# Two chained matrix products on one Trainium2 core: transposing x by DMA instead of TensorE, with the first products one block ahead

## The chip, the cores and the metric

The kernel runs on one core of one Trainium2 (trn2) chip. The metric is the device time of one execution in microseconds (us). The kernel before was run three times: median 1066.17 us (1066.07 to 1066.21). The profile is of one further execution, taken by the hardware profiler.

## The reference

```python
def setup_inputs():
    batch, m, k, h, n = 16, 512, 768, 3072, 768
    # x (batch, m, k), w1 (k, h), b1 (h), w2 (h, n), all float32, normally distributed

def reference(x, w1, b1, w2):
    y = np.matmul(x, w1) + b1
    y = np.maximum(y, 0)
    return np.matmul(y, w2).astype(np.float32)
```

x is taken as a matrix of 8192 rows by 768. The first product gives 8192 x 3072, bias and ReLU follow, and the second product gives 8192 x 768.

## The kernel before

The 8192 rows are worked in 16 blocks of 512. All operands are turned into bf16 while they are loaded, by DMAs from GpSimd's queue (POOL), which read fp32 in HBM and write bf16 in SBUF. Both weights stay in SBUF: `w1_sb` as 6 slices of 128 input features by 3072, `w2_sb` as 24 slices of 128 by 768. A row `w_sb` in the profile is either of them, `xl` is a loaded tile of x, 128 rows by 768 (196.6 KB in bf16; the profile writes 192 KB), four to a block.

TensorE multiplies along the partitions, so x is needed with its features on the partitions. `transpose_xblock` makes that tile, `xt`: for each of the four `xl` of a block it issues six TensorE transposes of 128 x 128 against the identity `ident` into a PSUM tile `trp` (two buffers), and VectorE (DVE) copies each `trp` into `xt`. In a block that is 24 transposes and 4 copies.

`mm1(xt)` makes 24 groups of 128 output features. A group is 6 matmuls of 128 x 512 into a PSUM tile `mm1p` (two buffers), and ScalarE (ACT) adds the bias, applies ReLU and writes bf16 into `yt`. A block has 144 of these matmuls. `mm2(blk, yt)` makes four groups of 128 rows. Each runs over the 24 slices of `w2_sb`, two matmuls of 128 x 384 a slice, into two PSUM tiles `mm2p`; DVE copies both into `osb`, and SyncE's queue (SP) stores `osb` to HBM. A block has 192 of these matmuls.

The loads of x run two blocks ahead of their use. At the start POOL issues x of block 0, the first six column pieces of w1 (128 columns each), x of block 1, the other 18 pieces of w1, and 24 pieces of w2. There are eight semaphores for POOL's DMAs, used in turn, so that the ninth issue waits for the first to land; the same holds for SP's DMAs with eight of their own. A scheduler sets each engine's order from the order of the code, and may draw single steps forward: in the kernel before it puts one of a block's four transposed tiles into the block ahead of it. Each engine's queue then runs strictly in that order.

The code and its line numbers in the profile:

Of the kernel before, what the change touches and what calls it, by code (L numbers as in the profile page):

```python
# [1 line left out]

# [5 lines left out]

FP32 = mybir.dt.float32
BF16 = mybir.dt.bfloat16  # L10


@with_exitstack
def kernel(
    ctx: ExitStack,
    tc: tile.TileContext,
    x: bass.AP,
    w1: bass.AP,
    b1: bass.AP,
    w2: bass.AP,  # L20
    out: bass.AP,
):
    nc = tc.nc
    P = 128

    xf = x.flatten_outer_dims()
    of = out.flatten_outer_dims()
    M, K = xf.shape
    K2, H = w1.shape
    H2, N = w2.shape  # L30
    assert K2 == K and H2 == H

    KS = K // P
    HS = H // P
    M_BLK = 512
    MSUB = M_BLK // P
    NBLK = M // M_BLK
    NF = 384
    NH = N // NF

    const_pool = ctx.enter_context(tc.tile_pool(name="const", bufs=1))
    w1_sb = const_pool.tile([P, KS, H], BF16)
    w2_sb = const_pool.tile([P, HS, N], BF16)
    b1_sb = const_pool.tile([P, HS], FP32)
    ident = const_pool.tile([P, P], BF16)

    make_identity(nc, ident)

    xload_pool = ctx.enter_context(tc.tile_pool(name="xload", bufs=8))
    xt_pool = ctx.enter_context(tc.tile_pool(name="xt", bufs=3))  # L50
    yt_pool = ctx.enter_context(tc.tile_pool(name="yt", bufs=2))
    osb_pool = ctx.enter_context(tc.tile_pool(name="osb", bufs=6))

    tr_psum = ctx.enter_context(tc.tile_pool(name="trps", bufs=2, space=bass.MemoryType.PSUM))
    mm1_psum = ctx.enter_context(tc.tile_pool(name="mm1ps", bufs=2, space=bass.MemoryType.PSUM))
    mm2_psum = ctx.enter_context(tc.tile_pool(name="mm2ps", bufs=4, space=bass.MemoryType.PSUM))

    w1r = w1.rearrange("(ko ki) h -> ki ko h", ki=P)

    def load_xblock(blk):  # L60
        m0 = blk * M_BLK
        xls = []
        for ms in range(MSUB):
            xl = xload_pool.tile([P, K], BF16, name="xl")
            nc.gpsimd.dma_start(  # L65
                out=xl, in_=xf[m0 + ms * P: m0 + (ms + 1) * P, :])
            xls.append(xl)
        return xls

    def transpose_xblock(xls):  # L70
        xt = xt_pool.tile([P, KS, M_BLK], BF16, name="xt")
        for ms in range(MSUB):
            trp = tr_psum.tile([P, KS, P], BF16, name="trp")
            for k in range(KS):
                nc.tensor.transpose(trp[:, k, :],  # L75
                                    xls[ms][:, k * P:(k + 1) * P], ident)
            nc.vector.tensor_copy(out=xt[:, :, ms * P:(ms + 1) * P], in_=trp)  # L77
        return xt

    def load_w1(ht0, ht1):  # L80
        for ht in range(ht0, ht1):
            nc.gpsimd.dma_start(out=w1_sb[:, :, ht * P:(ht + 1) * P],  # L82
                                in_=w1r[:, :, ht * P:(ht + 1) * P])

    def load_w2(h0, h1):
        for h in range(h0, h1):
            nc.gpsimd.dma_start(out=w2_sb[:, h, :],  # L87
                                in_=w2[h * P:(h + 1) * P, :])

    def mm1(xt):  # L90
        yt = yt_pool.tile([P, HS, M_BLK], BF16, name="yt")
        for ht in range(HS):
            ps = mm1_psum.tile([P, M_BLK], FP32, name="mm1p")
            for k in range(KS):
                nc.tensor.matmul(ps,  # L95
                                 lhsT=w1_sb[:, k, ht * P:(ht + 1) * P],
                                 rhs=xt[:, k, :],
                                 start=(k == 0), stop=(k == KS - 1))
            nc.scalar.activation(out=yt[:, ht, :], in_=ps,  # L99
                                 func=mybir.ActivationFunctionType.Relu,  # L100
                                 bias=b1_sb[:, ht:ht + 1])
        return yt

    def mm2(blk, yt):
        m0 = blk * M_BLK
        for ms in range(MSUB):
            osb = osb_pool.tile([P, N], FP32, name="osb")
            pss = [mm2_psum.tile([P, NF], FP32, tag="mm2", name="mm2p")
                   for _ in range(NH)]
            for h in range(HS):  # L110
                for j in range(NH):
                    nc.tensor.matmul(pss[j],  # L112
                                     lhsT=yt[:, h, ms * P:(ms + 1) * P],
                                     rhs=w2_sb[:, h, j * NF:(j + 1) * NF],
                                     start=(h == 0), stop=(h == HS - 1))
            for j in range(NH):
                nc.vector.tensor_copy(out=osb[:, j * NF:(j + 1) * NF],  # L117
                                      in_=pss[j])
            nc.sync.dma_start(out=of[m0 + ms * P: m0 + (ms + 1) * P, :],
                              in_=osb)  # L120

    xls0 = load_xblock(0)
    nc.sync.dma_start(out=b1_sb, in_=b1.rearrange("(t p) -> p t", p=P))
    load_w1(0, 6)
    xls1 = load_xblock(1)
    load_w1(6, HS)
    load_w2(0, HS)

    xls_next = [xls0, xls1]
    for blk in range(NBLK):  # L130
        xls = xls_next.pop(0)
        xt = transpose_xblock(xls)
        if blk + 2 < NBLK:
            xls_next.append(load_xblock(blk + 2))
        yt = mm1(xt)
        mm2(blk, yt)


# [1 line left out]
_INS = ['x', 'w1', 'b1', 'w2']  # L140
_OUTS = [((16, 512, 768), 'float32')]


# [23 lines left out]
```

## Time and profile before

| | |
|---|---|
| median of three runs | 1066.17 us |
| span of the profiled execution, first to last instruction | 1066.0 us |
| PE (TensorE matmul) busy | 1033.2 us, 97% of the span |
| ACT busy | 265.2 us, 25% |
| DVE busy | 96.9 us, 9% |
| POOL busy | 67.1 us, 6% |
| DMA, mean over the span | 45 GB/s |

The span starts at the core's first instruction and ends after its last. PE is matmuls and transposes, PEld the loading of their stationary operands, which overlaps PE. Bytes of DMA are those written, so a load of x or of a weight reads twice as many from HBM. The mean duration of a matmul in the profile includes the time in which it overlaps its neighbours; the spacing of matmuls is the busy time of a group over its count. In a row of the timeline the first figure is the start, the second the length, and the brackets at the end say how long the engine had been idle and what ended that.

### The profile page before, as it was taken

To read this page: it belongs to the slowest core of one execution; us is meant where nothing else is said; L and a number is where in the kernel's file an instruction comes from. 1 tells how busy PE (TensorE), PEld (TensorE's weight loads), DVE (VectorE), ACT (ScalarE), POOL (GpSimd) and SP (SyncE) were. 2 spreads that over 40 slices of the span, in tenths; PEclk is the share of its full clock that TensorE was granted. 3 is DMA by queue.
4 is the path that set the end of the run, shared out by engine and by line. 5 is a ranking of instruction groups with operands and counts; after the bars stand their busy time and mean duration, and the time that the engine had idled before them with its cause. 6 is when DMAs were issued, how large, how long until landed. Compare 5 with 4: busy or idle time off the path is not lost.

```text
span 1066.0 us, 12515 instructions
## 1 busy us (share of the span) xinstructions
PE 1033.2 (97%) x5760; PEld 551.0 (52%) x5760; DVE 96.9 (9%) x192; ACT 265.2 (25%) x385; POOL 67.1 (6%) x118
## 2 busy tenths in 40 slices
PE   7889999999999999999999999999999999999998
PEld 3344554645546455454555545455464554545554
DVE  1011010110101101020010101101011010100101
ACT  3303205032140412305123050321404214041230
POOL 7510000000000000000000000000000000000000
PEclk9999999999999999999999999999999999999999
DMA  9962030120301202011020201203012020100001
GB/s 158 195 129 60 16 75 1 45 45 15 75 1 45 45 30 60 1 54 37 30 60 15 69 7 43 47 16 74 1 46 45 19 64 1 45 15 31 30 1 60
DMA packets 43844, 48.00 MB, mean 45 GB/s; under 512 B 24336, under 2 KB 35600, under 8 KB 43792
## 3 DMA queue, kind: packets, MB, share of 16 engines
q0 software_dynamic: 31488, 22.03, 14.2%
q1 hardware_dynamic: 12304, 25.18, 6.3%
q8 instruction: 45, 0.74, 0.3%
q14 instruction: 7, 0.06, 0.0%
HBM read 44.05 MB, written 25.17 MB: 65 GB/s over the span
## 4 chain that ended last, share of the span: by engine, by line
PE 91%; DMA 4%; DVE 3%; POOL 1%; issue 0%; DVEq 0%; POOLq 0%
PE mm2p L112 46%; PE mm1p L95 44%; DMA w_sb<-in_w_dram 4%; DVE osb L117 1%; DVE xt L77 1%; POOL w_sb L82 1%; PE trp L75 1%; POOL xl L65 0%; DVEq L162 0%; POOL ident masks.py:199 0%; POOL ident masks.py:197 0%; POOLq masks.py:199 0%; POOLq L151 0%
## 5 line engine op out<-in xcount | busy, mean ns | idle before, releaser
L112 PE MATMUL mm2p<-w_sb,yt 128*128 128x384 bf16 x3072 | 506.2, 327 | 6.8 <-DMA w_sb<-in_w_dram 6.3
L95 PE MATMUL mm1p<-xt,w_sb 128*128 128x512 bf16 x2304 | 502.1, 380 | 3.9 <-DVE xt L77 3.9
L99 ACT ACTIVATE yt<-mm1p,b_sb 128x512 bf16<-128x512 f32 x384 | 263.9, 687 | 759.6 <-PE mm1p L95 759.6
L112 PEld LDWEIGHTS <-yt 128*128 128x128 bf16 x3072 | 301.1, 98 | 211.0 <-issue 12.3
L95 PEld LDWEIGHTS <-w_sb 128*128 128x128 bf16 x2304 | 225.7, 98 | 275.4 <-issue 8.1
L117 DVE COPY osb<-mm2p 128x384 f32<-128x384 f32 x128 | 65.3, 551 | 945.0 <-PE mm2p L112 945.0
L65 POOL DMA_DIRECT2D xl<-in_x_dram x64 | 34.1, 538 | 785.5 <-PE trp L75 780.4
L75 PE MATMUL trp<-ident,xl 128*128 128x128 bf16 x384 | 30.2, 224 | 17.6 <-DVE xt L77 11.2
L75 PEld LDWEIGHTS <-xl 128*128 128x128 bf16 x384 | 24.8, 100 | 23.6 <-issue 13.0
L77 DVE COPY xt<-trp 128x768 bf16<-128x768 bf16 x64 | 32.8, 549 | 20.4 <-PE trp L75 18.6
L82 POOL DMA_DIRECT2D w_sb<-in_w_dram x24 | 19.7, 836 | 5.2 <-DMA w_sb<-in_w_dram 4.6
L87 POOL DMA_DIRECT2D w_sb<-in_w_dram x24 | 12.7, 531 | 10.7 <-DMA w_sb<-in_w_dram 10.7
L99 ACT ACT_TABLE_LOAD x1 | 1.3, 1283 | 6.1 <-DMA b_sb<-in_b_dram 6.1
masks.py:199 POOL TENSOR_SCALAR_AFFINE_SELECT ident<-ident 128x128 bf16<-128x128 bf16 x1 | 0.3, 306 | 0.1
masks.py:197 POOL MEMSET ident<- 128x128 bf16 x1 | 0.2, 205 | 0.3 <-POOLq L151 0.3
L151 POOL MEMSET const-float32-0.0<- 128x1 f32 x1 | 0.1, 99 | 0.2 <-issue 0.2
L151 POOL MEMSET const-bfloat16-1.0<- 128x1 bf16 x1 | 0.1, 103 | 0.0
L151 POOL MEMSET const-uint8-127<- 128x1 uint8 x1 | 0.1, 103 | 0.0
L151 POOL MEMSET const-float32-1.0<- 128x1 f32 x1 | 0.1, 99 | 0.0
## 6 DMA issues: line engine op xcount, KB each, us to landing
out_dram<-osb SPq DMA_DIRECT2D x64, 384.0 KB, 2.3
xl<-in_x_dram POOLq DMA_DIRECT2D x64, 192.0 KB, 5.3
w_sb<-in_w_dram POOLq DMA_DIRECT2D x48, 192.0 KB, 7.8
b_sb<-in_b_dram SPq DMA_DIRECT2D x1, 12.0 KB, 5.3
```

The costliest lines, as they stand in the source:

```text
L65: nc.gpsimd.dma_start(out=xl, in_=xf[m0 + ms * P: m0 + (ms + 1) * P, :])
L75: nc.tensor.transpose(trp[:, k, :], xls[ms][:, k * P:(k + 1) * P], ident)
L77: nc.vector.tensor_copy(out=xt[:, :, ms * P:(ms + 1) * P], in_=trp)
L82: nc.gpsimd.dma_start(out=w1_sb[:, :, ht * P:(ht + 1) * P], in_=w1r[:, :, ht * P:(ht + 1) * P])
L87: nc.gpsimd.dma_start(out=w2_sb[:, h, :], in_=w2[h * P:(h + 1) * P, :])
L95: nc.tensor.matmul(ps, lhsT=w1_sb[:, k, ht * P:(ht + 1) * P], rhs=xt[:, k, :], start=(k == 0), stop=(k == KS - 1))
L99: nc.scalar.activation(out=yt[:, ht, :], in_=ps, func=mybir.ActivationFunctionType.Relu, bias=b1_sb[:, ht:ht + 1])
L112: nc.tensor.matmul(pss[j], lhsT=yt[:, h, ms * P:(ms + 1) * P], rhs=w2_sb[:, h, j * NF:(j + 1) * NF], start=(h == 0), stop=(h == HS - 1))
L117: nc.vector.tensor_copy(out=osb[:, j * NF:(j + 1) * NF], in_=pss[j])
L151: nc = _bacc.Bacc("TRN2", target_bir_lowering=False, num_devices=1)
```

## The change

Four things are changed:

- x of blocks 1 to 15 is transposed by `dma_start_transpose` on SP's queue, from `xl` in SBUF to `xt` in SBUF, four DMAs of 128 x 768 a block. Block 0 is still transposed on TensorE.
- The loop issues `mm1` of block b ahead of `mm2` of block b-1. `yt` has three buffers instead of two.
- w1 is loaded in pieces of 128, 128, 256 and five times 512 columns, all ahead of x of block 1; w2 in six pieces of four slices.
- The x loads and their transposes are still written two blocks ahead of their use.

```diff
-    yt_pool = ctx.enter_context(tc.tile_pool(name="yt", bufs=2))
+    yt_pool = ctx.enter_context(tc.tile_pool(name="yt", bufs=3))
...
+    def xbar_xblock(xls):
+        xt = xt_pool.tile([P, KS, M_BLK], BF16, name="xt")
+        for ms in range(MSUB):
+            nc.sync.dma_start_transpose(
+                out=xt[:, :, ms * P:(ms + 1) * P], in_=xls[ms])
+        return xt
...
     def load_w1(ht0, ht1):
-        for ht in range(ht0, ht1):
-            nc.gpsimd.dma_start(out=w1_sb[:, :, ht * P:(ht + 1) * P],
-                                in_=w1r[:, :, ht * P:(ht + 1) * P])
+        nc.gpsimd.dma_start(out=w1_sb[:, :, ht0 * P:ht1 * P],
+                            in_=w1r[:, :, ht0 * P:ht1 * P])
+
+    w2r = w2.rearrange("(t p) n -> p t n", p=P)
 
     def load_w2(h0, h1):
-        for h in range(h0, h1):
-            nc.gpsimd.dma_start(out=w2_sb[:, h, :],
-                                in_=w2[h * P:(h + 1) * P, :])
+        nc.gpsimd.dma_start(out=w2_sb[:, h0:h1, :], in_=w2r[:, h0:h1, :])
...
     xls0 = load_xblock(0)
     nc.sync.dma_start(out=b1_sb, in_=b1.rearrange("(t p) -> p t", p=P))
-    load_w1(0, 6)
+    load_w1(0, 1)
+    load_w1(1, 2)
+    load_w1(2, 4)
+    for ht in range(4, HS, 4):
+        load_w1(ht, ht + 4)
     xls1 = load_xblock(1)
-    load_w1(6, HS)
-    load_w2(0, HS)
+    for h in range(0, HS, 4):
+        load_w2(h, h + 4)
 
-    xls_next = [xls0, xls1]
-    for blk in range(NBLK):
-        xls = xls_next.pop(0)
-        xt = transpose_xblock(xls)
-        if blk + 2 < NBLK:
-            xls_next.append(load_xblock(blk + 2))
-        yt = mm1(xt)
-        mm2(blk, yt)
+    xts = [transpose_xblock(xls0), xbar_xblock(xls1)]
+    yts = [None] * NBLK
+    for blk in range(NBLK + 1):
+        if blk < NBLK:
+            if blk + 2 < NBLK:
+                xts.append(xbar_xblock(load_xblock(blk + 2)))
+            yts[blk] = mm1(xts[blk])
+        if blk >= 1:
+            mm2(blk - 1, yts[blk - 1])
```

On PE, at the end of a block's second products: in the kernel before, the last two matmuls of `mm2` of block 0 and the first transpose of an `xl` of block 1 (the numbers tell buffers apart).

```order
L112 LDWEIGHTS yt_193
L112 MATMUL mm2p_549<-w2_sb_59,yt_193 128x384
L112 LDWEIGHTS yt_193
L112 MATMUL mm2p_550<-w2_sb_59,yt_193 128x384
L75 LDWEIGHTS xl_104
L75 MATMUL trp_611<-ident_61,xl_104 128x128
```

In the changed kernel, the same two matmuls of `mm2` of block 0 (`yt_169`), and behind them the first of `mm1` of block 2 (`xt_164`).

```order
L118 LDWEIGHTS yt_169
L118 MATMUL mm2p_731<-w2_sb_59,yt_169 128x384
L118 LDWEIGHTS yt_169
L118 MATMUL mm2p_732<-w2_sb_59,yt_169 128x384
L101 LDWEIGHTS w1_sb_58
L101 MATMUL mm1p_798<-xt_164,w1_sb_58 128x512
```

What moved: no transpose and no wait for one of DVE's copies stands between the two kinds of matmul any more; the `LDWEIGHTS` of L101 waits for the four DMAs that fill `xt_164`.

Also on PE, at the end of `mm1` of block 0 in the changed kernel (`xt_118` is x of block 0, `xt_151` that of block 1):

```order
L101 LDWEIGHTS w1_sb_58
L101 MATMUL mm1p_354<-xt_118,w1_sb_58 128x512
L101 LDWEIGHTS w1_sb_58
L101 MATMUL mm1p_376<-xt_151,w1_sb_58 128x512
L101 LDWEIGHTS w1_sb_58
```

In the kernel before, `mm2` of block 0 stands in the place of `mm1p_376`; now `mm1` of block 1 follows at once, and the four DMA transposes of block 1 are due there.

On POOL, the loads at the start, as a difference (`-` before, `+` changed):

```order
 L65 DMA xl<-in_x_dram 128x768 x3
-L82 DMA w_sb<-in_w_dram 128x6x128 x6
+L88 DMA w_sb<-in_w_dram 128x6x128 x2
+L88 DMA w_sb<-in_w_dram 128x6x256
+L88 DMA w_sb<-in_w_dram 128x6x512 x5
 L65 DMA xl<-in_x_dram 128x768 x4
-L82 DMA w_sb<-in_w_dram 128x6x128 x18
-L87 DMA w_sb<-in_w_dram 128x768 x24
+L94 DMA w_sb<-in_w_dram 128x4x768 x6
 L65 DMA xl<-in_x_dram 128x768 x56
```

What moved: x of block 1 (the four `xl` in the middle) now stands behind all of w1 instead of behind a quarter of it.

On SP, the queue before was one load of b1 and the 64 stores. In the changed kernel it begins:

```order
L131 DMA b_sb<-in_b_dram 128x24x1
L73 DMA_TRANSPOSE xt<-xl 128x6x128 x16
L125 DMA out_dram<-osb 128x768 x4
L73 DMA_TRANSPOSE xt<-xl 128x6x128 x4
L125 DMA out_dram<-osb 128x768 x4
```

What moved: the transposes of blocks 1 to 4 stand ahead of the first store, and from there four transposes alternate with four stores. Each waits for its `xl` to land; the first of a block also waits for the `mm1` that last read its `xt` buffer.

## Prediction, made before the changed kernel was run

> **What bounds the kernel now.** I read the page's head and its groups first, then the chain of work that ended last, then the timeline at one block boundary, and then the start with the DMA rates, because there the changed kernel has a new deadline. The head and the groups:
>
> ```profile
> span 1066.0 us, 12515 instructions
> PE 1033.2 (97%) x5760; PEld 551.0 (52%) x5760; DVE 96.9 (9%) x192; ACT 265.2 (25%) x385; POOL 67.1 (6%) x118
> ...
> L112 PE MATMUL mm2p<-w_sb,yt 128*128 128x384 bf16 x3072 | 506.2, 327 | 6.8 <-DMA w_sb<-in_w_dram 6.3
> L95 PE MATMUL mm1p<-xt,w_sb 128*128 128x512 bf16 x2304 | 502.1, 380 | 3.9 <-DVE xt L77 3.9
> ...
> L75 PE MATMUL trp<-ident,xl 128*128 128x128 bf16 x384 | 30.2, 224 | 17.6 <-DVE xt L77 11.2 <-DMA xl<-in_x_dram 6.2
> ```
>
> PE is the bound. The two products take 1008 us of it; the transposes take 30.2 us, and PE is idle 17.6 us just before them. The chain gives the rhythm of a middle block (start, length, what), and its last row the last second product:
>
> ```profile
> 349.01 31.24 PE mm1p L95 x144
> 380.25 31.05 PE mm2p L112 x191
> 411.32 1.02 DVE osb L117 x2
> 413.39 0.57 DVE xt L77
> 414.00 31.24 PE mm1p L95 x144
> ...
> 1030.20 31.05 PE mm2p L112 x191
> ```
>
> From 349.01 to 414.00 a block takes 64.99 us. The boundary close up:
>
> ```profile
> 411.28 0.83 PE L75 MATMUL trp<-ident,xl 128*128 128x128 bf16 x12
> 412.86 0.96 PE L75 MATMUL trp<-ident,xl 128*128 128x128 bf16 x12 [0.74 <-DVE xt L77]
> 414.00 4.26 PE L95 MATMUL mm1p<-xt,w_sb 128*128 128x512 bf16 x19 [0.18 <-DVE xt L77]
> ```
>
> The second products run from 380.25 to 411.28 (31.03 us), then the transposes and their waits for DVE take until 414.00, which is 2.72 us a block in which no product runs. The start has its own losses:
>
> ```profile
> 10.00 0.10 PEld L95 LDWEIGHTS <-w_sb 128*128 128x128 bf16 x1 [0.56 <-DMA w_sb<-in_w_dram]
> 10.36 10.05 PE L95 MATMUL mm1p<-xt,w_sb 128*128 128x512 bf16 x36 [0.65 <-DVE xt L77]
> 17.86 0.69 ACT L99 ACTIVATE yt<-mm1p,b_sb 128x512 bf16<-128x512 f32 x1 [0.61 <-PE mm1p L95]
> 20.25 0.50 PE L75 MATMUL trp<-ident,xl 128*128 128x128 bf16 x6
> 20.61 19.60 PE L95 MATMUL mm1p<-xt,w_sb 128*128 128x512 bf16 x90
> 43.92 2.70 PE L112 MATMUL mm2p<-w_sb,yt 128*128 128x384 bf16 x14
> 62.37 24.10 PE L112 MATMUL mm2p<-w_sb,yt 128*128 128x384 bf16 x137 [1.32 <-DMA w_sb<-in_w_dram]
> 89.02 1.24 PE L95 MATMUL mm1p<-xt,w_sb 128*128 128x512 bf16 x5 [0.18 <-DVE xt L77]
> ```
>
> Block 0's second products start at 43.92 and creep behind the w2 pieces until 62.37; block 1 starts at 89.02, 45.1 us after 43.92, where 31.03 + 2.72 would do.
>
> ```profile
> 0.00:5.00 5.00, 0.00 (x0) 0.00 (x0) 0.00 (x0) 0.00 (x0) 4.05 (x12) 1.00 0.59 41
> 5.00:10.00 5.00, 3.29 (x24) 2.23 (x25) 1.93 (x4) 1.28 (x1) 4.89 (x7) 1.00 1.36 180
> 25.00:30.00 5.00, 5.00 (x25) 2.29 (x24) 0.00 (x0) 2.57 (x5) 3.29 (x4) 1.00 1.82 181
> 50.00:55.00 5.00, 2.81 (x13) 1.18 (x13) 0.00 (x0) 0.00 (x0) 2.70 (x6) 1.00 1.16 207
> 60.00:65.00 5.00, 3.54 (x14) 1.62 (x13) 0.91 (x2) 0.00 (x0) 0.46 (x1) 0.75 1.16 207
> 65.00:70.00 5.00, 5.00 (x30) 2.90 (x28) 0.11 (x1) 0.00 (x0) 0.00 (x0) 0.91 0.45 123
> ```
>
> These are stretches of 5 us; the last three figures are the granted PE clock, the DMA share and GB/s written. Loads run at 181 GB/s while w1 comes in rows of 256 bytes, at 207 while w2 comes in rows of 1536. From 25 to 30 us PE is full beside that traffic, so DMA does not slow its matmuls. After the thin stretch the clock drops (0.75, then 0.91), which costs 5 x 0.25 + 5 x 0.09 = 1.7 us.
>
> **The change, part by part.** The sum is made against the profiled span, 1066.0 us; the median of the runs lies 0.2 above it.
>
> First products of block 0. Their order and first loads stay, so they start at 10.36, with the same slow first matmuls. The hoisted transposes between 20.25 and 20.61 go (0.36 us), so they end at 43.92 - 0.36 = 43.56. The larger w1 pieces could delay them: the fourth piece (columns 4 to 7 of the 24 groups) is needed when the fourth group is done, about 17.6 (its ACT row starts at 17.86). By 10 us 5 x 41 + 5 x 180 = 1105 KB had come; x of block 0 and the first three pieces are 8 tiles' worth, 1573 KB, so they are in at 12.6 by 180 GB/s, and the next 786 KB at 16.4 by 207 or 16.9 by 181. The first w1 piece was byte-wise in at 9.3 and released PE at 10.0, so 0.7 is added: 17.1 to 17.6. That just holds, and the later pieces gain on PE (3.8 to 4.3 us each against 5.2 us of matmuls). I take 0; ends 0 and +1.
>
> x of block 1, and its transposes: this is the term that decides. PE wants `xt` of block 1 at 43.56. All of w1 and x of block 1 are 6.29 MB, in by 12.6 + 4.72 MB / 207 + 0.7 = 36.1 for the last `xl`, and 2.8 earlier, 33.3, for the first. (At 181 GB/s the last lands at 39.4.) The trace before has no DMA transpose. The rows nearest to it:
>
> ```profile
> out_dram<-osb SPq DMA_DIRECT2D x64, 384.0 KB, 2.3
> xl<-in_x_dram POOLq DMA_DIRECT2D x64, 192.0 KB, 5.3
> w_sb<-in_w_dram POOLq DMA_DIRECT2D x48, 192.0 KB, 7.8
> b_sb<-in_b_dram SPq DMA_DIRECT2D x1, 12.0 KB, 5.3
> ...
> q1 hardware_dynamic: 3088, 0.01, 5.5%
> ```
>
> (The last row is SP's queue over the first 33 us: the b1 load.) In shape the nearest is a w1 piece: as many bytes as an `xl`, in 768 runs of 256 bytes, which is one 128-column row of a transposed square. At 181 GB/s it holds the DMA engines 1.09 us; in landing the nearest is the store, which leaves SBUF by SP's queue in 2.3. Beside it the w2 load keeps the engines full, and I let the two share them evenly: 4 x 2 x 1.09 = 8.7 us from 33.3, so 42.0, and 2.3 to land: 44.3. The wait is 44.3 - 43.56 = 0.8 us. Low end: no sharing, 36.1 + 1.09 + 2.3 = 39.5, no wait. High end: one tile at a time, each as long as a queued load, 33.3 + 4 x 7.8 = 64.5, a wait of 20.9 and the 1.7 of clock on top, 22.6. I take 0.8, by the shape. [...]
>
> Second products of block 0 now start 31.24 later, at 75.6. The w2 load ends where it did or sooner (62.37 before; the transposes take some 4 to 5 us of the engines from it), so the waits and the clock drop go: the cover is the first products of block 1. [...]
>
> Steady blocks. 24 transposes, 4 DVE copies and PE's waits for them go: 2.72 a block. The DMA transposes of block b+2 can start when first products of block b-1 end, and are wanted some 155 us later (five runs of 31 us), so 4 x 7.8 = 31 us would be hidden too. On SP the stores of block b stand behind the transposes of block b+4, which wait for the end of `mm1` of block b+1; PE runs that right ahead of `mm2` of block b, so no store waits for it. DVE's copies and ACT have no new work. POOL waits for transposes before it refills an `xl`: 155 us of slack again. The three `yt` buffers are needed by the new order; cost 0. At each first product PE waits on four DMA semaphores instead of DVE; I take 0, ends 0 and 0.24 a block, the 3.9 us over 16 blocks in the group row of L95.
>
> The tail stays: the last second products start at 1030.20, 31.03 later is 1061.23, the span ends 4.77 later.
>
> The sum: 43.56 + 0.8 + 15 x 31.24 + 16 x 31.03 + 4.77 = 43.56 + 0.8 + 468.6 + 496.5 + 4.8 = 1014.2 us of span, 1014.4 as a median. Against before that is -51.8: 15 x 2.72 = 40.8 at the boundaries, and the rest at the start.
>
> **Rivals.** 1. The transposes come one after the other and PE stands at 43.56 once. For it: SP has never carried more than one DMA at a time here, the engines are full then, and the b1 row shows that 12 KB on SP's queue took 5.3 us beside loads. Against it: the stores, 2.3. With 5.3 a tile (the x row) 33.3 + 21.2 = 54.5, so a wait of 10.9 and 1.7 of clock: 1013.4 + 12.6 + 0.2 = 1026; with 7.8 it is 1036. [...]
>
> 2. Slower: the DMA bound takes PE's place in every block. It decides from the time of a tile in a full stream, t: first products of block 15 would start at 33.3 + 60 t, and 31.24 + 2 x 31.03 + 4.77 follow; that reaches 1066 at t = 15.6 us. It would be so if a transpose moved single elements. The b1 load moved 3088 packets in 5.5% of 33 us on 16 engines, 9.4 ns each; 98,304 elements of a tile are then 57.8 us, and the kernel takes about 3600 us. Against it: runs of 256 bytes are there to be moved whole.
>
> 3. The order pays less: a bubble of 0.24 us at each first product (four semaphores), 1018.
>
> That the order is not what the change says can't be: in the program's rows no transpose stands between products.
>
> **How the numbers follow.** The forecast, a wait of at most 4 us at block 1 and clean boundaries, is 0.62, with its own range 1013 to 1018. Rival 1 has 0.25 (1018 to 1036), rival 3 0.08, rival 2 0.03, something unforeseen that eats the gain 0.02. The range goes from 1012.5 to 1036: below it only the wait can shrink and 1 us of the start's timing, above it rival 2 is left out. A measurement of this kernel can tell about 0.2% (2 us) from no change. Faster is 0.62 + 0.25 + 0.08 and part of the unforeseen, 0.96; same 0.01; slower 0.03.
>
> **What the profile after would show.** No L75 row between products and a period of 62.3 us in the chain; PE waiting for w2 nowhere; the wait at the first product of block 1 (at 43 to 45 us) as the size of the deciding term, with the landing of `xt<-xl` in the DMA issues beside 2.3 and 7.8. If that landing is over 15 us in the steady part, or PE waits for `xt` in more than one block, the forecast is wrong in kind; if the matmul spacing itself rises above 31.24 and 31.03 us a block, what I said of DMA beside matmuls was wrong.

## The result: 26 us faster, with 21.5 us lost at one wait

The changed kernel takes 1039.71 us (median of 4, 1039.05 to 1040.52) against 1066.19 for the kernel before, a ratio of 0.9752 (95% interval 0.9738 to 0.9766). Forecast were 1014.4 and a range up to 1036.0, so the sign was right and the time lies above the range.

The head of the page after, SP's and GpSimd's DMA queues (packets, MB, share of 16 engines), the groups of the two products and the DMA issues:

```profile
span 1038.3 us, 11851 instructions
PE 1004.9 (97%) x5400; PEld 529.3 (51%) x5400; DVE 67.6 (7%) x132; ACT 265.1 (26%) x385; POOL 45.7 (4%) x84
...
q0 software_dynamic: 18656, 22.03, 14.3%
q1 hardware_dynamic: 60304, 36.99, 14.1%
...
L101 PE MATMUL mm1p<-xt,w_sb 128*128 128x512 bf16 x2304 | 504.7, 382 | 22.1 <-DMA xt<-xl 21.5
L118 PE MATMUL mm2p<-w_sb,yt 128*128 128x384 bf16 x3072 | 501.7, 326 | 0.0
...
xt<-xl SPq DMA_TRANSPOSE x60, 4.3
```

The transposes are gone from between the products, and so is every wait for w2 (0.0 before L118). In their place stands one wait of 21.5 us for `xt`. The chain of work that ended last shows where (start, length, what):

```profile
39.75 6.50 SPq L73
46.25 0.04 issue
46.29 19.75 DMA xt<-xl
66.05 0.14 issue
66.18 33.49 PE mm1p L101 x144
99.67 31.20 PE mm2p L118 x192
130.87 31.08 PE mm1p L101 x144
161.95 31.20 PE mm2p L118 x192
193.15 31.08 PE mm1p L101 x144
```

From 130.87 to 193.15 a block takes 62.28 us, as forecast (62.27). The loss is nearly all at block 1. SP issues its four transposes at 34.27, 35.65, 39.75 and 46.29; they land 11.3, 16.9, 19.6 and 19.8 us later, one after the other some 7 us apart, the last at 66.05. The timeline of PE there, and three stretches of 5 us:

```profile
10.83 33.85 PE L101 MATMUL mm1p<-xt,w_sb 128*128 128x512 bf16 x144 [0.65 <-DVE xt L84]
66.18 33.49 PE L101 MATMUL mm1p<-xt,w_sb 128*128 128x512 bf16 x144 [21.50 <-DMA xt<-xl]
...
55.00:60.00 5.00, 0.00 (x0) 0.00 (x0) 0.00 (x0) 0.00 (x0) 0.67 (x2) 0.50 1.17 202
65.00:70.00 5.00, 3.82 (x10) 1.34 (x11) 0.00 (x0) 0.69 (x1) 0.53 (x1) 0.50 1.19 206
70.00:75.00 5.00, 5.00 (x23) 2.23 (x22) 0.00 (x0) 2.06 (x3) 0.53 (x1) 0.92 1.33 157
```

The first products of block 0 end at 10.83 + 33.85 = 44.68. The next begin 21.5 us later on a halved clock (0.50), so they take 33.49 instead of 31.08, another 2.4 us. All the while the DMA engines write 202 GB/s. What do they write? The two queues in the stretch from 40 to 46 us:

```profile
q0 software_dynamic: 696, 1.04, 94.8%
q1 hardware_dynamic: 695, 0.17, 21.9%
```

As many packets of the one as of the other. It stays so in the next three stretches of 6 us, and 0.3 us is as even (34 and 35 from 50.0 on), so a turn here was one packet or very few. SP's late fourth issue therefore left no gap in the queue. From 40 to 64 us 2797 of the 3200 packets pass that the four transposes have: from the two pages, (60304 - 12304) / 60 = 800 a tile, with (36.99 - 25.18) MB / 60 = 197 KB; in the trace 768 of the 800 are rows of 256 bytes, 32 have 4 bytes. The kernel before had these on SP's queue:

```profile
q1 hardware_dynamic: 12304, 25.18, 6.3%
```

A w2 packet is one row of 1536 bytes (1.04 MB in 696 packets). So the transposes got every second packet, but only a seventh of the bytes (0.17 of 1.21 MB). 6 us x 16 engines / 695 is 138 ns for a pair; 200 pairs an engine make 27.6 us. In the trace it is 27.9, from the first packet at 38.1 to the landing at 66.05.

### The profile page after: what moved, and what is told of

The parts are those of the page before. It is cut to its first block, busy times and chain, and to the rows that moved or that the text cites. A ratio compares the mean times of both kernels' runs of the same rounds, so it can differ in the third digit from the quotient of the medians.

```text
span 1038.3 us, 11851 instructions
## 1 busy us (share of the span) xinstructions
PE 1004.9 (97%) x5400; PEld 529.3 (51%) x5400; DVE 67.6 (7%) x132; ACT 265.1 (26%) x385; POOL 45.7 (4%) x84
## 3 DMA queue, kind: packets, MB, share of 16 engines
q1 hardware_dynamic: 60304, 36.99, 14.1%
## 4 chain that ended last, share of the span: by engine, by line
PE 93%; DMA 4%; SPq 1%; POOL 1%; issue 0%; DVE 0%; DVEq 0%; POOLq 0%
PE mm2p L118 48%; PE mm1p L101 45%; DMA xl<-in_x_dram 2%; DMA xt<-xl 2%; SPq L73 1%; POOL w_sb L88 1%; POOL xl L65 0%; DVE osb L123 0%; DVEq L175 0%; POOL ident masks.py:199 0%; POOL ident masks.py:197 0%; POOLq masks.py:199 0%; POOLq L164 0%
## 5 line engine op out<-in xcount | busy, mean ns | idle before, releaser
L101 PE MATMUL mm1p<-xt,w_sb 128*128 128x512 bf16 x2304 | 504.7, 382 | 22.1 <-DMA xt<-xl 21.5
L118 PE MATMUL mm2p<-w_sb,yt 128*128 128x384 bf16 x3072 | 501.7, 326 | 0.0
L118 PEld LDWEIGHTS <-yt 128*128 128x128 bf16 x3072 | 300.6, 98 | 200.2
L101 PEld LDWEIGHTS <-w_sb 128*128 128x128 bf16 x2304 | 226.5, 98 | 296.4 <-issue 28.9
L82 PE MATMUL trp<-ident,xl 128*128 128x128 bf16 x24 | 3.3, 310 | 6.9 <-DMA xl<-in_x_dram 6.8
L88 POOL DMA_DIRECT2D w_sb<-in_w_dram x8 | 6.6, 874 | 0.0
L82 PEld LDWEIGHTS <-xl 128*128 128x128 bf16 x24 | 2.2, 138 | 7.7 <-DMA xl<-in_x_dram 7.7
L94 POOL DMA_DIRECT2D w_sb<-in_w_dram x6 | 4.5, 743 | 13.7 <-DMA w_sb<-in_w_dram 13.3
L84 DVE COPY xt<-trp 128x768 bf16<-128x768 bf16 x4 | 2.2, 557 | 8.6 <-PE trp L82 8.6
```

The source lines that it names most:

```text
L82: nc.tensor.transpose(trp[:, k, :], xls[ms][:, k * P:(k + 1) * P], ident)
L88: nc.gpsimd.dma_start(out=w1_sb[:, :, ht0 * P:ht1 * P], in_=w1r[:, :, ht0 * P:ht1 * P])
L94: nc.gpsimd.dma_start(out=w2_sb[:, h0:h1, :], in_=w2r[:, h0:h1, :])
L101: nc.tensor.matmul(ps, lhsT=w1_sb[:, k, ht * P:(ht + 1) * P], rhs=xt[:, k, :], start=(k == 0), stop=(k == KS - 1))
L118: nc.tensor.matmul(pss[j], lhsT=yt[:, h, ms * P:(ms + 1) * P], rhs=w2_sb[:, h, j * NF:(j + 1) * NF], start=(h == 0), stop=(h == HS - 1))
```

## The experiments

Theory A: the DMA engines alternate packet by packet between the two queues. Theory B: a transpose is slow in itself, and SP takes one at a time (rival 1 of the prediction). Theory C, the step in the sum: two loads share the engines evenly by time or bytes.

**The row length of w2 (1536, 768, 256 bytes).** Bytes, number of DMAs and their place stay.

```diff
-    for h in range(0, HS, 4):
-        load_w2(h, h + 4)
+    for c in range(0, N, 128):        # w2_rows128
+        nc.gpsimd.dma_start(out=w2_sb[:, :, c:c + 128], in_=w2r[:, :, c:c + 128])
+    for h in range(0, HS, 8):         # w2_rows384, in its place
+        for c in range(0, N, 384):
+            nc.gpsimd.dma_start(out=w2_sb[:, h:h + 8, c:c + 384],
+                                in_=w2r[:, h:h + 8, c:c + 384])
```

> The changed kernel, with w2 loaded in six pieces of eight slices by 384 columns: the same bytes and number of DMAs, packets of 768 bytes. Theory A (packet by packet): a pair of packets takes about 82 ns an engine, 200 of them 16.4 us, the transposes land at about 53 us and the wait at block 1 is 7 to 10 us, between those of 256 and 1536 bytes. Theories B and C: near 21 us.

> The changed kernel, with w2 loaded in six pieces of all 24 slices by 128 columns instead of four slices by 768: the same bytes and the same number of DMAs in the same places, but packets of 256 bytes instead of 1536. Theory A (packet by packet): a pair of packets takes 40 to 55 ns an engine instead of 138, the 200 transpose packets of an engine take 8 to 11 us, the transposes land at 45 to 48 us and the wait at block 1 is 0 to 4 us. Theory B (slow in itself): the wait stays near 21 us. Theory C (the engines are shared by time or bytes, so only the load's total matters): the wait stays as it was, near 21 us, or grows, since the shorter rows load more slowly.

One run each: 1029.40 us with 768 bytes, 1022.13 with 256. The queues from 40 to 44 us and PE's first row of block 1, with 768 bytes:

```profile
q0 software_dynamic: 758, 0.58, 92.0%
q1 hardware_dynamic: 759, 0.19, 36.2%
...
55.45 33.53 PE L101 MATMUL mm1p<-xt,w_sb 128*128 128x512 bf16 x141 [11.16 <-DMA xt<-xl]
```

The same with 256 bytes:

```profile
q0 software_dynamic: 1368, 0.35, 84.7%
q1 hardware_dynamic: 1366, 0.33, 64.9%
...
48.78 32.93 PE L101 MATMUL mm1p<-xt,w_sb 128*128 128x512 bf16 x141 [4.50 <-DMA xt<-xl]
```

The packets are even again, and a pair takes 4 us x 16 / 758 = 84 ns and 47 ns. The wait falls from 21.5 to 11.2 and 4.5 us, though the transposes are the same and the load has the same bytes. That is A; B and C both put it near 21. Each wait is somewhat above what was expected (7 to 10, 0 to 4), and one thing explains it: beside loads the first packet of a transpose moved about 4 us after its issue (issued at 34.0 to 34.3 in these three runs; first packet at 38.10 in the trace of the changed kernel, and at an estimated 38.0 and 38.5 in the other two, counted back from the 375 and 494 packets through by 40 us at 84 and 47 ns a pair), and an estimated 1.3 us after it on a quieter queue (below). From 38.1, 200 pairs end at 65.7, 54.9 and 47.5; the products start at 66.18, 55.45 and 48.78.

**w2 held back until the transposes have landed.** A GpSimd copy of a few elements reads `xt` of block 1 and writes where the w2 loads write later, so GpSimd's queue waits there; four more do it for x of block 2.

```diff
+    xts = [transpose_xblock(xls0), xbar_xblock(xls1)]
+    nc.gpsimd.tensor_copy(out=w2_sb[:, 0:HS:4, 0:4],
+                          in_=xts[1][:, :, 0:M_BLK:P])
     for h in range(0, HS, 4):
         load_w2(h, h + 4)
 
-    xts = [transpose_xblock(xls0), xbar_xblock(xls1)]
...
+            if gate is not None:      # block 2 only: gate = xts[1]
+                nc.gpsimd.tensor_copy(out=xl[:, 0:4], in_=gate[:, 0, 0:M_BLK:P])
             nc.gpsimd.dma_start(out=xl, ...)
```

> The changed kernel, but the w2 loads and the x loads of block 2 are held back until the four DMA transposes of block 1 have landed (a small GpSimd copy reads their result and writes into the first columns of the tiles that the loads fill afterwards). Theory A (the DMA engines alternate packet by packet between the two queues, so a transpose's 256-byte packets wait behind w2's 1536-byte packets): beside the last x tiles only, 30 packets an engine at 0.138 us and 170 at 0.025 us, so the transposes land at 44 to 46 us, the wait at block 1 falls from 21.5 to under 2 us, and the span is 1014 to 1017 us. Theory B (a transpose is slow in itself, one after the other on SP's queue, 6 us each at the start): the wait stays over 15 us and the span over 1030 us.

1015.10 us (median of 4), 0.952 of the kernel before (0.9504 to 0.9536). Its page, the GpSimd copy in its timeline, SP's queue from 36 to 40 us, and PE:

```profile
span 1013.0 us, 11809 instructions
...
40.89 0.22 POOL L142 COPY w_sb<-xt 128x24 bf16<-128x24 bf16 x1 [22.99 <-DMA xt<-xl]
...
q1 hardware_dynamic: 2561, 0.63, 84.5%
q0 software_dynamic: 4, 0.00, 0.7%
...
10.31 64.01 PE L104 MATMUL mm1p<-xt,w_sb 128*128 128x512 bf16 x282 [0.65 <-DVE xt L87]
```

With the other queue nearly empty, 2561 packets move in 4 us, one every 25 ns on an engine. SP's issues may set that pace, 1.32 us for the first tile (the changed kernel moves 1145 transpose packets from 74 to 75 us, when several tiles are queued and no load runs: one in 14 ns). All four tiles have landed at 40.9, earlier than the 44 to 46 expected and before PE wants them. The two runs of first products go through without a gap from 10.31. B is out: the same 60 DMAs, issued by the same queue. It is the fastest of all versions run.

**x of block 1 loaded earlier, behind half of w1.** Its transposes then run beside rows of 1024 bytes.

```diff
-    for ht in range(4, HS, 4):
-        load_w1(ht, ht + 4)
+    load_w1(4, 8)
+    load_w1(8, 12)
     xls1 = load_xblock(1)
+    for ht in range(12, HS, 4):
+        load_w1(ht, ht + 4)
```

> The changed kernel with x of block 1 loaded after the first 12 of the 24 column groups of w1 instead of after all of them. By packet alternation the transposes now run beside w1's packets of 1024 bytes (about 0.1 us a pair and engine): 200 packets an engine take some 20 us from 23 on, so they land at 43 to 46 us, and w1's later pieces come slower, which costs the first products of block 0 up to 3 us: time 1016 to 1021 us. If a transpose beside any load takes what it took in the changed kernel (7 us a tile), the wait is 5 us or more and the time over 1022.

1024.30 us (ratio 0.9604, 0.9589 to 0.9618): better than the change as made, and 3 us above what was expected. The queues from 34 to 38 us and two rows of PE:

```profile
q0 software_dynamic: 628, 0.63, 92.7%
q1 hardware_dynamic: 631, 0.15, 29.9%
...
29.53 5.35 PE L101 MATMUL mm1p<-xt,w_sb 128*128 128x512 bf16 x23 [1.44 <-DMA w_sb<-in_w_dram]
50.76 1.87 PE L101 MATMUL mm1p<-xt,w_sb 128*128 128x512 bf16 x4 [5.11 <-DMA xt<-xl]
```

The pair takes 4 x 16 / 630 = 102 ns as expected. But of the first issue at 22.1 no packet had moved by 26.0 (598 had by 30), and w1's rows ended at an estimated 39.4 us (507 packets and 0.67 MB of the load from 38 to 42 us are some 210 rows of 1024 bytes and 290 of 1536), when some 1970 of the 3200 packets were through (1758 by 38); the others ran beside w2's long rows. The over-1022 outcome had been put to "7 us a tile beside any load"; the pair shows that this is not why.

**Block 1 on TensorE.** Only blocks 2 to 15 are transposed by DMA.

```diff
-    xts = [transpose_xblock(xls0), xbar_xblock(xls1)]
+    xts = [transpose_xblock(xls0), None]
...
             yts[blk] = mm1(xts[blk])
+            if blk == 0:
+                xts[1] = transpose_xblock(xls1)
```

> The changed kernel, but block 1 too is transposed on TensorE, behind the first products of block 0; blocks 2 to 15 stay with the DMA. Theories A, B and C agree here: the 21.5 us wait and the slow clock behind it go (1038.3 - 21.5 - 2.4 = 1014.4), 24 transposes and their waits for VectorE come back once (2.7 us): 1017 us. If the wait only moves to block 2 (its transposes also run beside the w2 load), the span stays above 1025 us.

1017.15 us (ratio 0.9537, 0.9523 to 0.9552), span 1014.7. In all of PE's waits the first products wait for an `xt` once, at block 0, and never for a DMA transpose:

```profile
PE mm1p L101 <- DVE xt L84: 0.6, 1, 0.6
```

The wait at block 1 is gone and does not move to block 2.

**Which part of the change does what.** The DMA transposes with the loop's old order; the new order with TensorE transposes; the new loads alone in the kernel before.

```diff
     # dma_old_order: the loop's body
+        mm2(blk, mm1(xts[blk]))
     # tensore_new_order: ahead of mm1 in the loop, instead of the DMA transposes
+            xt = transpose_xblock(xls[blk])
     # loads_only: the kernel before, with load_w1, load_w2 and their calls as changed
```

> The changed kernel with the loop's old order: second products of block b stand behind first products of block b, ahead of those of block b+1. DMA transposes, loads and buffers stay. If the reordering is what put the transposes of block 1 on the path (they are now wanted only after the second products of block 0), no product waits for a transpose; instead the second products of block 0 creep behind the w2 load again, which the transposes slow: w2 done near 64 us, first products of block 1 at 89 to 92, then 15 blocks of 62.28: a span of 1026 to 1030 us and a time of 1027 to 1032, some 10 us faster than the changed kernel as it was made. If the transposes were slow for a reason of their own, the first products of block 1 would still wait for them and the time would be 1035 or more.

1030.84 us (0.9666, 0.9651 to 0.9680), as expected. No product waits for a DMA transpose; the second products wait for w2:

```profile
PE mm2p L118 <- DMA w_sb<-in_w_dram: 9.1, 5, 3.1
```

With the DMA transposes, the new order as it was made thus costs 1039.7 - 1030.8 = 8.9 us: it takes away the cover of block 1's transposes, 31 us of second products.

> The changed kernel with all blocks transposed on TensorE, in the new order and with the new loads. What the order and the loads are worth without the DMA transposes: nothing waits for w2, and 15 boundaries cost 2.72 us each again: 1014.4 + 40.8 = 1055 us of span, 1053 to 1058 us of time; less if the scheduler finds better places for the transposes.

1036.89 us (0.9725, 0.9709 to 0.9741), 16 us below what was expected. The chain at one of its boundaries:

```profile
141.31 29.41 PE mm2p L118 x181
170.72 0.67 PE trp L82 x12
171.39 0.81 PE mm2p L118 x5
172.20 0.42 PE trp L82 x6
172.62 0.16 PE mm2p L118
172.79 0.34 PE trp L82 x6
173.12 0.81 PE mm2p L118 x5
173.94 0.23 PE mm1p L101
```

The scheduler now has second products to put between the transposes, and they cover the waits for DVE. Its next second products start at 205.03, so a block takes 205.03 - 141.31 = 63.72 us: of the 2.72 us of a boundary, 1.27 go by the order alone, and only 1.44, which is 24 transposes of 60 ns, need the DMA. 15 x 1.44 = 21.6 is what separates this version from w2_after_xt1 (1036.9 - 1015.1 = 21.8). The change as made, 1039.7, is not faster than its own order with TensorE transposes.

> The kernel before with the changed loads alone (w1 in pieces of 128, 128, 256 and 512 columns ahead of x of block 1, w2 in six pieces). If w1 at 207 GB/s instead of 181 brings the end of w2 forward by 3 us and the second products of block 0 wait for that end, the time is 1062 to 1065 us; if larger pieces make PE wait longer for each, 1066 or more.

1067.80 us (ratio 1.0011, 1.0001 to 1.0020): the gain of 1.3 to 4.3 us that the first branch expected did not come, and the second branch's 1066 or more did. PE's last row behind the w2 load:

```profile
59.02 26.48 PE L111 MATMUL mm2p<-w_sb,yt 128*128 128x384 bf16 x152 [1.04 <-DMA w_sb<-in_w_dram]
```

The load does end 3.3 us sooner (62.37 before), but coming in fours it leaves 152 matmuls to do instead of 137, 15 x 0.16 = 2.4 us. The waits for it are fewer and longer, and their sum is the same (6.3 us, 4 waits instead of 13). Block 1 starts at 88.52 instead of 89.02; why the timed runs are 1.5 us longer all the same is not shown.

## Why the prediction was wrong, step by step

- **The step that failed** is "I let the two share them evenly", 8.7 us for four transposes. The engines shared by packets, 695 against 696, and a packet of the load is six times as long (1536 bytes against 256). Measured: 27.9 us, beside the same w2 load. Of the 21.7 us from the forecast landing at 44.3 to 66.05 this makes 19.2. The sum also let the first packet move at once, where it came 3.8 us after the issue; the first issue came 1.0 us late; and the 2.3 us that were added for landing do not show. The duration of a tile alone, 1.09 us from a w1 piece, was about right: 800 packets at 14 to 25 ns on 16 engines are 0.7 to 1.25 us. The sum had used bytes and time.
- Rival 1 gave 20.9 us of wait and 1036, near what came. Its picture was right, tiles that land one after the other and PE standing once; its reason was not. SP had issued three before the first had landed (45.6), and what made each take some 7 us was the queue being let through one packet in two. Its price, 7.8 us from the landing of a queued load, was right by chance: w2_after_xt1 shows all four tiles landed 7 us after the first issue.
- What put it above the range's 1036: the first products of block 0 ended at 44.68 instead of 43.56 (1.1 us; they began 0.5 later, and the slow matmuls of the start, 0.43 us apart, went on until 16.25 instead of 14.58), the wait was 21.5 instead of 20.9, and the clock cost 2.4 instead of 1.7. Together 2.4 us of span. The other 1.2 us are the step from span to time: 0.2 was added, from a profiled execution of the kernel before that was a long one (1066.0; the timed runs of it beside the experiments had spans of 1064.0 to 1065.0 and times 1.9 to 2.1 above them). Here it is 1.8 in one and the same run (1040.09 and 1038.3).
- Right: the period (62.28 against 62.27), no wait for w2, stores and x loads off the path, no bubble at the four semaphores (rival 3: 0), rival 2 far off (a tile in a free stream took at most 1.25 us, 800 packets at 25 ns on 16 engines, against the 15.6 that would decide). The sum without the wait, 1013.4 of span, is what w2_after_xt1 reached: 1013.0. (The 6.29 MB of the prediction are w1 and x of both first blocks; the sum made with them is right.)
- How long PE has to wait for its clock to drop, the runs do not give as one figure. By estimates from the mean clock of the stretches it fell to 0.50 some 2.2 us into the wait in the changed kernel (0.94 from 46 to 47 us, 0.50 from 47 on) and in w2_rows384 (0.65 from 45 to 50 us), and in w2_rows128 at 49.7, behind the whole wait of 4.5 us (0.97 from 45 to 50 us, 0.69 from 50 to 55). After 5.1 us (x1_earlier) the first matmuls stood 0.42 us apart, where 31.08 / 144 = 0.22 is the spacing in a middle block. In the kernel before the longest wait for w2 was 1.32 us, and the drop (0.75 from 60 to 65 us) came behind a row of them; in loads_only the clock was 0.50 from 55 to 60 us, behind waits of 1.5, 2.3 and 1.6 us.
- The 40.8 us at the boundaries were booked to the DMA transposes; tensore_new_order shows that the order alone brings 15 x 1.27 = 19 of them.

## What to carry to other kernels

When a DMA with short rows has a deadline beside a bulk load in another queue, count packets as well as bytes: here it got one packet for each of the load's (695 against 696), so its time was its packets per engine times the time of a pair (200 x 138 ns = 27.6 us, measured 27.9), and some 4 us more before the first. Two ways out worked here: to keep the bulk load back until it was through (1015.1 us), or to move the deadline (1030.8 with the old order); shorter rows in the load helped too (1029.4 and 1022.1). And before a transpose is taken off TensorE, see what its waits cost in the best order: about half of the gain at the boundaries (19 of 40.8 us) needed only other matmuls to stand beside it.

## What the runs showed of the hardware that was not expected

- The time of a pair rose with the load's row: 47, 84, 102 and 138 ns for 256, 768, 1024 and 1536 bytes written, by a line through these an estimated 29 ns + 0.071 ns a byte, where transpose packets alone took 14 ns with several tiles queued (1145 from 74 to 75 us), and came every 25 ns in w2_after_xt1 (2561 in 4 us).
- Beside a full load queue the first packet of a transpose moved 3.8 us after its issue in the changed kernel (34.27 and 38.10), and by estimates from the packet counts 3.9 to 4.4 us in the three runs with other rows beside it; with three x tiles left in the queue (w2_after_xt1, issue at 33.90, 485 packets by 36 us at 25 ns), an estimated 1.3 us. Why was not tried.
- SP was held by a transpose: 6.50 us for one issue beside the w2 load (the chain above), against 1.24 in the median of the 60.
